# Splits on VectorE, shared gate splits, an early next segment and an earlier sum split in a one-core encoder layer

## The chip, the core and the metric

The kernel runs on one core of a Trainium2 chip. The metric is device time in microseconds (us) of one execution. The kernel before took 3487.39 us as the median of 3 runs (3483.35 to 3494.15).

The engines: TensorE (PE in the profile; its weight loads are PEld), VectorE (DVE), ScalarE (ACT), GpSimd (POOL) and SyncE (SP), which issues most DMAs. Each runs its own list of instructions in order; semaphores join them.

## The reference, cut to what matters

One encoder layer over 2048 tokens of width 1024, in float32:

```python
h = rmsnorm(x, ln_mix[layer])
z = h @ w_in[layer]
q_a, f_fw, f_bw, i_a, og_a, c_q, c_kv, k_rope, gate_a, gate_b = jnp.split(z, split_points, axis=-1)
...
o_hg = hgrn_direction(f_fw, lb_all[0, layer], False) + hgrn_direction(f_bw, lb_all[1, layer], True)
y_a = o_hg.reshape(B, S, HG_V).astype(x.dtype) @ w_oA[layer]
...
o_mla = block_dense_attention(qm, km, vm)     # 8 heads, softmax over all 2048 keys
y_b = o_mla @ w_oB[layer]
merged = jax.nn.sigmoid(gate_a) * y_a + jax.nn.sigmoid(gate_b) * y_b
x = x + merged @ w_out[layer]
x = x + hierarchical_moe(rmsnorm(x, ln_moe[layer]), ...)
x = x + (p[layer] @ w_ple_proj[layer]) * jax.nn.sigmoid(rmsnorm(x, ln_ple[layer]) @ w_ple_gate[layer])
```

`hgrn_direction` is a gated linear recurrence over the sequence, 4 heads of 128 x 128 state, run forwards and backwards.

## The kernel before

A product in full precision is made of three TensorE passes: each operand is split into a rounded high part and a low part (high x high, high x low, low x high). A split is one ScalarE copy (the high part) and one subtract (the low part) on VectorE or GpSimd. The order of every engine is written out by hand: inside `manual_schedule` an engine gets its instructions in the order in which the Python code emits them, and generators (`yield`) interleave strands of work.

**Stage 1, `stage_in`** (about 0 to 696 us) computes z but for the two branch gates. `todo` lists, for each of 4 token blocks (512 tokens), 5 groups of 288 columns done in 4 slots each (tokens by columns, `grp` is a number) and 6 groups of 256 columns done in 2 slots each (`grp` is None). A slot is 24 matmuls. Behind a slot's matmuls come: `post()` of the slot before (ScalarE, sometimes a VectorE product L346/L369 that reads PSUM), one step of every lane in `lanes` (`norm` of the next token block; `mla_block`, which normalises and rotates the latent q and k: lines L423 to L520), and in slot 0 `split_raw`, the split of the next group's weights in two halves (`whi` on ScalarE L269, `wlo` L270 on GpSimd). `load_raw` then starts the group after that.

**Stage 2, `hgrn` with `gates`** (about 696 to 1293 us). 16 segments (4 heads x 4 blocks of 512 tokens). `hgrn_levels` runs a segment in 8 steps: the start (`ff` L611 on ScalarE, `kk` L613 and `qq` L615 on VectorE, then matmuls L620/L621 into `h_ps`), and 7 levels. A level is: `h_ku` = copy of half of `kk` (ScalarE L627), `h_at` under a mask (VectorE L629), `kk` times `ff` in place (VectorE L632), half of the new `h_qq` (GpSimd L634), the other half copied (VectorE L635), `ff` pairs multiplied (VectorE L637), then matmuls L641. `hgrn_tail` (per segment) and `hgrn_forward` (per head: sums over the 4 segments, a reciprocal root in some 13 small VectorE steps, the scaled `h_so` L733, its transposes L737 into `h_pf`) are side strands; `side()` moves each of them by one step between a step's elementwise work and its matmuls.

`gates` is the filler: 64 units (4 token blocks x 16 column blocks of 128), each 24 matmuls L791 of 512 columns with its own weights `g_wr` loaded, split (`g_wh` on ScalarE, `g_wl` on GpSimd L768), and a sigmoid stored. It yields twice per GATE_STEP = 8 matmuls; each step of `hgrn` takes two yields. What is left of it runs on in the last `while tails` loop, in the start of `attention` (`run(n)`, between the first row maxima) and, in one piece, in `more()`.

**Stage 3, `attention`** (about 1361 to 2168 us; its first maxima run from 1314 us). 32 blocks (8 heads x 4 blocks of 512 queries) of 16 steps `kt`; a step is 3 score matmuls, 2 value matmuls, and 2 for the row maxima of the next block in every other step (`max_step`: 2 matmuls into `t_pm`, one PSUM buffer, then a VectorE reduction L947). Softmax sums of the first 12 key blocks are added up on GpSimd in `t_za` (L978, L980); `sums0` copies their high part to `t_zh` (ScalarE L1004) in step 13, `sums1` makes the low part `t_zl` (GpSimd L1009) in step 14, and `sums2` (step 15) multiplies both (L1015, L1016).

The merge, the experts and the last gate follow; the change does not touch them.

Of the kernel before, what the change touches and what calls it, by code (L numbers as in the profile page):

```python
# [174 lines left out]
def stage_in(tc, g, x, positions, ln_mix, w_in, qa_norm, kva_norm, w_uq, w_ukv, q_norm, k_norm, late):  # L175
# [5 lines left out]
    with ExitStack() as es:  # L181
# [199 lines left out]
        for at, (tb, c0, n, grp) in enumerate(todo):  # L381
# [5 lines left out]
            for i in range(2 if grp is None else 4):  # L387
# [18 lines left out]
                if i == 0 and at + 1 < len(todo):  # L406
                    ws = split_raw(raws, todo[at + 1][2], (nc.gpsimd if at + 2 < len(todo) else nc.vector,) * 2)
# [195 lines left out]
def hgrn_levels(tc, g, work, psum, hd, seg, loaded, z):  # L603

    nc = tc.nc
# [7 lines left out]
    nc.vector.tensor_scalar(kk, ff[:, 0:2], -1.0, 1.0, op0=OP.mult, op1=OP.add)  # L613
    qq = work.tile([128, 2, TB], F32, name="h_qq", bufs=5)
    nc.vector.tensor_tensor(qq, q[:, None, :].to_broadcast([128, 2, TB]), ff[:, 1:3], op=OP.mult)  # L615
    yield
    ps = psum.tile(SH, F32, name="h_ps")
    for c in range(HC):
        cs = slice(c * 128, (c + 1) * 128)
        nc.tensor.matmul(ps[:, c], kk[:, 0, cs], q[:, cs], start=True, stop=False)  # L620
        nc.tensor.matmul(ps[:, c], kk[:, 1, cs], q[:, cs], start=False, stop=True)  # L621
    yield
    at = work.tile(SH, F32, name="h_at")
    for lv in range(7):
# [10 lines left out]
        nc.vector.tensor_copy(others(qn, h, TB), others(qq, h, TB))  # L635
# [12 lines left out]
def hgrn_tail(tc, g, work, psum, hd, seg, z, st):  # L648
# [50 lines left out]
def hgrn_forward(tc, g, work, psum, hd, st):  # L699
# [4 lines left out]
    for seg in range(NTB):  # L704
# [29 lines left out]
        yield  # L734
        pt = psum.tile(SH, F32, name="h_pf", bufs=1)
# [8 lines left out]
def gates(tc, g, work, psum, w_in, n):  # L744

    nc = tc.nc
    todo = [(tb, cb) for tb in reversed(range(NTB)) for cb in range(2 * KC)]

    def raw(at, queue=nc.sync):
        if at >= len(todo):  # L750
            return None
        c0 = C_G + todo[at][1] * 128
# [18 lines left out]
    hx = None  # L771
# [9 lines left out]
    for at, (tb, cb) in enumerate(todo):
        if cb == 0:
            hx, hn = hn, []
        if cb in (4, 6, 8, 10) and tb:
            hn.append(row(tb - 1, len(hn) % 2, len(hn) // 2 * 4))
        pm = psum.tile([128, TB], F32, name="g_pm")
        wn = None
        for k in range(KC):
            a, b = (w[0][:, k], w[1][:, k]), (hx[k // 4 * 2][:, k % 4], hx[k // 4 * 2 + 1][:, k % 4])
            for i, (x, y) in enumerate(((a[0], b[0]), (a[0], b[1]), (a[1], b[0]))):  # L790
                nc.tensor.matmul(pm, x, y, start=k == 0 and i == 0, stop=k == KC - 1 and i == 2)  # L791
                count += 1
                if count % n == 0:
                    yield
                    if post:
                        post()
                        post = None
# [1617 lines left out]
```

## Time and profile before

| | us |
|---|---|
| median of 3 runs | 3487.39 (3483.35 to 3494.15) |
| the profiled execution | 3486.7, of which the span from first to last instruction is 3484.9 |
| TensorE busy | 3319.5 (95% of the span) |
| VectorE, ScalarE, GpSimd busy | 2489.9, 1985.3, 1435.8 |

Stages by their windows: 696 us for stage 1, 544 us for the 16 segments (696 to 1240), 121 us up to the first scores (1361), 807 us of attention, 1316 us for all that follows. [...]

### The profile page before, as it was taken

To read this page: it belongs to the slowest core of one execution; us is meant where nothing else is said; L and a number is where in the kernel's file an instruction comes from. 1 tells how busy PE (TensorE), PEld (TensorE's weight loads), DVE (VectorE), ACT (ScalarE), POOL (GpSimd) and SP (SyncE) were. 2 spreads that over 40 slices of the span, in tenths; PEclk is the share of its full clock that TensorE was granted. 3 is DMA by queue.
4 is the path that set the end of the run, shared out by engine and by line. 5 is a ranking of instruction groups with operands and counts; after the bars stand their busy time and mean duration, and the time that the engine had idled before them with its cause. 6 is when DMAs were issued, how large, how long until landed. Compare 5 with 4: busy or idle time off the path is not lost. (4 is left out here: it accounts for less than half of the span.)

```text
span 3484.9 us, 48287 instructions
## 1 busy us (share of the span) xinstructions
PE 3319.5 (95%) x16784; PEld 2784.7 (80%) x16784; DVE 2489.9 (71%) x4334; ACT 1985.3 (57%) x3522; POOL 1435.8 (41%) x973
## 2 busy tenths in 40 slices
PE   7999999999899899999999999999979999999899
PEld 6898989888787787777777777788868887888687
DVE  5545343388898854888888887665569998999775
ACT  5454544444444435888888887112228887888522
POOL 3333333255444435878777776000002222222244
PEclk9999999999999899999999999999989999999999
DMA  5645554554444354111101001876559899999642
GB/s 162 220 148 178 158 192 123 194 158 122 133 134 123 123 153 148 29 27 29 30 22 29 21 14 41 256 207 232 191 192 339 335 327 343 380 359 362 227 170 109
DMA packets 345077, 587.09 MB, mean 168 GB/s; under 512 B 57503, under 2 KB 220607, under 8 KB 332542
## 3 DMA queue, kind: packets, MB, share of 16 engines
q1 hardware_dynamic: 323726, 538.96, 46.4%
q0 software_dynamic: 20688, 43.45, 3.4%
q8 instruction: 133, 2.18, 0.3%
q10 hardware_dynamic: 416, 1.57, 0.1%
q14 instruction: 114, 0.93, 0.1%
HBM read 470.47 MB, written 146.93 MB: 177 GB/s over the span
## 5 line engine op out<-in xcount | busy, mean ns | idle before, releaser
L1919 DVE TENSOR_TENSOR e_wl<-e_raw,e_wh 128x1024 fp32r<-128x1024 f32 x384 | 459.7, 1221 | 47.9 <-ACT e_wh L1917 39.4
L980 POOL TENSOR_TENSOR t_za<-t_za,t_ph 128x512 f32<-128x512 f32 x320 | 416.0, 1300 | 47.8 <-ACT t_ph L972 34.8
L1917 ACT ACTIVATE e_wh<-e_raw 128x1024 fp32r<-128x1024 f32 x384 | 402.8, 1068 | 21.5 <-DMA e_raw<-in_w_dram 17.6
L270 POOL TENSOR_TENSOR wlo<-wraw,whi 128x1024 fp32r<-128x1024 f32 (+1 forms) x85 | 223.2, 2648 | 439.7 <-ACT whi L269 439.7
L947 DVE TENSOR_REDUCE t_mx<-t_pm 128x1 f32<-128x1024 f32 x256 | 313.4, 1224 | 118.2 <-PE t_pm L946 116.9
L985 DVE TENSOR_TENSOR t_pl<-t_ps,t_ph 128x512 fp32r<-128x512 f32 x512 | 341.9, 683 | 54.6 <-ACT t_ps L973 50.8
L972 ACT ACTIVATE t_ph<-t_ps 128x512 fp32r<-128x512 f32 x512 | 304.9, 596 | 111.9 <-PE t_ps L970 100.5
L791 PE MATMUL g_pm<-g_h,g_wh 128*128 128x512 f32 x1024 | 341.5, 407 | 1.9 <-ACT g_wh L767 1.9
L973 ACT ACTIVATE t_ps<-t_ps 128x512 f32<-128x512 f32 x512 | 303.3, 592 | 0.0
L1971 POOL DMA_INDIRECT d_y<-e_raw,sly x64 | 75.3, 1176 | 466.0 <-ACT e_raw L1969 404.6
L634 POOL TENSOR_TENSOR h_qq<-h_qq,h_ff 128x512 f32<-128x512 f32 x112 | 152.7, 1363 | 200.3 <-DVE h_ff L637 116.0
L791 PEld LDWEIGHTS g_pm<-g_h,g_wh 128*128 128x128 f32 x1024 | 194.6, 194 | 38.4 <-ACT g_wh L767 2.2
L768 POOL TENSOR_TENSOR g_wl<-g_wr,g_wh 128x1024 fp32r<-128x1024 f32 x63 | 153.9, 2443 | 141.1 <-ACT g_wh L767 133.7
L99 PE MATMUL e_pg<-e_wh,e_xh 128*128 128x512 f32 x512 | 208.9, 408 | 1.7 <-ACT e_wh L1917 1.2
L791 PE MATMUL g_pm<-g_h,g_wl 128*128 128x512 f32 x512 | 208.9, 408 | 1.6 <-POOL g_wl L768 1.1
L99 PE MATMUL pm<-whi,hh 128*128 128x288 f32 x640 | 198.4, 310 | 11.2 <-DVE qo L346 9.6
L968 PE MATMUL t_ps<-t_ql,t_kh 96*128 96x512 f32 x512 | 205.0, 400 | 2.0 <-DVE t_pl L985 2.0
L627 ACT ACTIVATE h_ku<-h_kk 128x512 f32<-128x512 f32 x112 | 75.6, 675 | 228.6 <-DVE h_kk L632 190.8
L100 PE MATMUL e_pg<-e_wl,e_xh 128*128 128x512 f32 x512 | 202.2, 395 | 2.9 <-DVE e_wl L1919 2.6
L101 PE MATMUL e_pg<-e_wh,e_xl 128*128 128x512 f32 x512 | 204.1, 399 | 0.5 <-DVE e_xl L1906 0.5
L997 PE MATMUL t_pa<-t_ph,vt 128*128 128x512 f32 x512 | 202.1, 395 | 0.0
L970 PE MATMUL t_ps<-t_qh,t_kh 97*128 97x512 f32 x512 | 202.0, 394 | 0.0
(452 smaller groups left out, 9356.9 us busy)
## 6 DMA issues: line engine op xcount, KB each, us to landing
e_raw<-in_w_dram SPq DMA_DIRECT2D x256, 512.0 KB
e_raw<-in_w_dram SPq DMA_DIRECT2D x64, 1024.0 KB
g_wr<-in_w_in_dram SPq DMA_DIRECT2D x62, 512.0 KB
wraw<-in_w_in_dram SPq DMA_DIRECT2D x48, 512.0 KB
wraw<-in_w_in_dram SPq DMA_DIRECT2D x40, 576.0 KB
d_g<-g_o SPq DMA_DIRECT2D x64, 256.0 KB
m_g<-d_g SPq DMA_DIRECT2D x64, 256.0 KB
p_y<-d_y SPq DMA_DIRECT2D x16, 1024.0 KB
```

What stands on the lines that cost most here:

```text
L99: nc.tensor.matmul(out, ah, bh, start=start, stop=False)
L101: nc.tensor.matmul(out, al, bh, start=False, stop=stop)
L270: e.tensor_tensor(lo[:, k:k + 4, :n], raw[:, :, :n], hi[:, k:k + 4, :n].bitcast(F32), op=OP.subtract)
L791: nc.tensor.matmul(pm, x, y, start=k == 0 and i == 0, stop=k == KC - 1 and i == 2)
L947: nc.vector.tensor_reduce(mx[n, i][:, j:j + 1], pm.rearrange("p a b -> p (a b)"), axis=AX, op=OP.max)
L968: nc.tensor.matmul(ps, kh[0:QK, ks], ql[0:QK], start=True, stop=False)
L972: nc.scalar.activation(ph, ps, AF.Exp)
L973: nc.scalar.activation(ps, ps, AF.Exp)
L980: nc.gpsimd.tensor_tensor(za[n], za[n], ph.bitcast(F32), op=OP.add)
L985: nc.vector.tensor_tensor(pl, p, ph.bitcast(F32), op=OP.subtract)
L1917: nc.scalar.activation(hi, raw, AF.Copy)
L1919: nc.vector.tensor_tensor(lo, raw, hi.bitcast(F32), op=OP.subtract)
```

## The change

1. `split_raw` becomes a generator of two steps and always subtracts on VectorE. In the 4-slot groups the first half is emitted in slot 0, the second in slot 1; in the 2-slot groups both in slot 0. At the start of the kernel the first group's second half and the second token tile's square sum are emitted earlier.
2. `gates` has a list `uses` of 40 weight blocks instead of 64: 12 column blocks used for the token blocks a and b together, then 4 for each of a, b, c, d alone, then 12 for c and d together. Rows of b are loaded at the start (by SP), those of c and d while the single ones run. GATE_STEP is 9, and both yields of a step are taken before `side()`.
3. `hgrn_levels` has more yields; the next segment's `ff`, `kk`, `qq` are emitted in steps 5, 6 and 7 of the segment before. Step 0 adds the two `kk` (VectorE) so that one matmul per block replaces the pair L620/L621. The other half of `h_qq` is copied on ScalarE. `hgrn_tail` gets a yield ahead of its products, `hgrn_forward` one between `h_so` and its transposes.
4. `sums0` and `sums1` move to steps 12 and 13.

```diff
-        def split_raw(raws, n, engines):
+        def split_raw(raws, n):
...
-            for raw, e, k in zip(raws, engines, range(0, KC, 4)):
+            for raw, k in zip(raws, range(0, KC, 4)):
                 nc.scalar.activation(hi[:, k:k + 4, :n], raw[:, :, :n], AF.Copy)
-                e.tensor_tensor(lo[:, k:k + 4, :n], raw[:, :, :n], hi[:, k:k + 4, :n].bitcast(F32), op=OP.subtract)
+                nc.vector.tensor_tensor(lo[:, k:k + 4, :n], raw[:, :, :n], hi[:, k:k + 4, :n].bitcast(F32), op=OP.subtract)
+                yield
             return hi, lo
...
                 if i == 0 and at + 1 < len(todo):
-                    ws = split_raw(raws, todo[at + 1][2], (nc.gpsimd if at + 2 < len(todo) else nc.vector,) * 2)
+                    part = split_raw(raws, todo[at + 1][2])
+                    next(part)
+                    if grp is None:
+                        ws = all_steps(part)
+                if i == 1 and grp is not None:
+                    ws = all_steps(part)
...
+    ks = work.tile([128, TB], F32, name="h_ku")
+    nc.vector.tensor_tensor(ks, kk[:, 0], kk[:, 1], op=OP.add)
     yield
     ps = psum.tile(SH, F32, name="h_ps")
     for c in range(HC):
         cs = slice(c * 128, (c + 1) * 128)
-        nc.tensor.matmul(ps[:, c], kk[:, 0, cs], q[:, cs], start=True, stop=False)
-        nc.tensor.matmul(ps[:, c], kk[:, 1, cs], q[:, cs], start=False, stop=True)
+        nc.tensor.matmul(ps[:, c], ks[:, cs], q[:, cs], start=True, stop=True)
...
-        nc.vector.tensor_copy(others(qn, h, TB), others(qq, h, TB))
+        nc.scalar.activation(others(qn, h, TB), others(qq, h, TB), AF.Copy)
...
             nc.vector.scalar_tensor_tensor(so[:, c], op[:, c], r[:, c:c + 1], so[:, c], op0=OP.mult, op1=OP.mult)
         yield
+        yield
         pt = psum.tile(SH, F32, name="h_pf", bufs=1)
...
-    todo = [(tb, cb) for tb in reversed(range(NTB)) for cb in range(2 * KC)]
+    a, b, c, d = reversed(range(NTB))
+    last = 2 * KC
+    uses = [(cb, (a, b)) for cb in range(last - 4)]
+    uses += [(cb, (t,)) for t in (a, b) for cb in range(last - 4, last)]
+    uses += [(cb, (t,)) for t in (c, d) for cb in range(4)]
+    uses += [(cb, (c, d)) for cb in range(4, last)]
...
     w, wr = parts(wr, nc.vector), wn
+    for i in range(4):
+        row(b, i)
     yield
...
         for step in range(8):
             next(lane)
-            for _ in range(5 if n == step == 0 else 1):
+            if step == 5 and n + 1 < len(segs):
+                nxt = begin(n + 1)
+            if step >= 5 and n + 1 < len(segs):
+                next(nxt[0])
+            for _ in range(6 if n == step == 0 else 2):
                 next(fill, None)
             side()
-            next(fill, None)
             next(lane, None)
...
-GATE_STEP = 8
+GATE_STEP = 9
...
+            if kt == 12:
+                sums0(n)
             if kt == 13:
-                sums0(n)
-            if kt == 14:
                 sums1(n)
```

What this moves, at three places. Stage 1, a 4-slot group, VectorE: two rotation steps of `mla_block` (L485 to L507, after the change L501 to L523; `kf` is what PE transposes next) with the `hl` splits of `norm` between them. Before:

```order
L206 TENSOR_TENSOR hl<-pt,hh 128x4x128 x2
L485 TENSOR_TENSOR qs<-qs,hr_y_4525 128x768
L486 TENSOR_TENSOR kf<-kf,hr_y_4525 128x8x64
L493 TENSOR_TENSOR ra<-qs,tc_899 128x256
L496 TENSOR_TENSOR rb<-qs,ts_900 128x8x16 x2
L498 TENSOR_TENSOR qs<-ra,rb 128x8x32
L502 TENSOR_TENSOR ka<-csb,tc_977 128x32
L504 TENSOR_TENSOR kb<-csb,ts_978 128x16 x2
L505 TENSOR_TENSOR ka<-ka,kb 128x32
L507 TENSOR_TENSOR kf<-ka,hr_y_4525 128x8x32
```

The same place after:

```order
L206 TENSOR_TENSOR hl<-pt,hh 128x4x128 x2
L270 TENSOR_TENSOR wlo<-wraw_4463,whi 128x4x256
L501 TENSOR_TENSOR qs<-qs,hr_y_4525 128x768
L502 TENSOR_TENSOR kf<-kf,hr_y_4525 128x8x64
L509 TENSOR_TENSOR ra<-qs,tc_899 128x256
L512 TENSOR_TENSOR rb<-qs,ts_900 128x8x16 x2
L514 TENSOR_TENSOR qs<-ra,rb 128x8x32
L518 TENSOR_TENSOR ka<-csb,tc_975 128x32
L520 TENSOR_TENSOR kb<-csb,ts_976 128x16 x2
L521 TENSOR_TENSOR ka<-ka,kb 128x32
L523 TENSOR_TENSOR kf<-ka,hr_y_4525 128x8x32
```

One half of a weight split (`wlo`) now stands in VectorE's row between the two rotations; it stood in GpSimd's before.

Stage 2, ScalarE, around the turn from one segment to the next (`h_op` and `h_qf` are a tail's copies, `g_o` and `g_wh` the gates'). Before:

```order
L691 ACTIVATE h_op<-h_po 128x512
L693 ACTIVATE h_qf<-h_qq 128x512
L627 ACTIVATE h_ku<-h_kk 128x512 x2
L809 ACTIVATE g_o<-g_pm 128x512
L767 ACTIVATE g_wh<-g_wr 128x1024
L627 ACTIVATE h_ku<-h_kk 128x512
L611 ACTIVATE h_ff<-h_sg,lb,lbc 128x512 x3
L627 ACTIVATE h_ku<-h_kk 128x512
L631 ACTIVATE h_at<-h_ps 128x512
```

After:

```order
L628 ACTIVATE h_ff<-h_sg,lb,lbc 128x512 x3
L714 ACTIVATE h_op<-h_po 128x512
L716 ACTIVATE h_qf<-h_qq 128x512
L649 ACTIVATE h_ku<-h_kk 128x512
L657 ACTIVATE h_qq<-h_qq 128x8x2x32
L846 ACTIVATE g_o<-g_pm 128x512
L804 ACTIVATE g_wh<-g_wr 128x1024
L649 ACTIVATE h_ku<-h_kk 128x512
L657 ACTIVATE h_qq<-h_qq 128x4x2x64
L846 ACTIVATE g_o<-g_pm 128x512
L649 ACTIVATE h_ku<-h_kk 128x512
L653 ACTIVATE h_at<-h_ps 128x512
```

`h_ff` of the next segment has moved three steps forward, and every level has a second ScalarE copy (L657), which waits for GpSimd's half of the same tile.

The start of attention, PE: the first row maxima (`t_pm`) of block 0 and the gate matmuls between them. Before:

```order
L791 MATMUL g_pm<-g_h,g_wl 128x512
L791 MATMUL g_pm<-g_h,g_wh 128x512
L946 MATMUL t_pm<-t_kh,t_qh 128x512 x2
L791 MATMUL g_pm<-g_h,g_wh 128x512
L791 MATMUL g_pm<-g_h,g_wl 128x512
L791 MATMUL g_pm<-g_h,g_wh 128x512 x2
```

After:

```order
L829 MATMUL g_pm<-g_h,g_wh 128x512 x2
L829 MATMUL g_pm<-g_h,g_wl 128x512
L993 MATMUL t_pm<-t_kh,t_qh 128x512 x16
L1002 MATMUL t_pb<-ident,mz_12566 97x128 x4
L993 MATMUL t_pm<-t_kh,t_qh 128x512 x6
L1015 MATMUL t_ps<-t_ql,t_kh 128x512
```

All of the gates' matmuls now stand ahead of the first maximum: 60 behind the last `h_pf` transposes, none behind the first `t_pm`. Before, 88 stood between those two, and 176 behind the first `t_pm`.

## Rows read from the trace of the kernel before

**Rows 1.** The page's first part: busy us of each engine, share of the span, instructions.
```profile
PE 3319.5 (95%) x16784; PEld 2784.7 (80%) x16784; DVE 2489.9 (71%) x4334; ACT 1985.3 (57%) x3522; POOL 1435.8 (41%) x973
```
**Rows 2.** [...]
```profile
30.00:696.00 666.00, 634.52 (x3712) 573.29 (x3712) 293.97 (x712) 303.28 (x647) 220.05 (x94) 0.97 0.52 171
696.00:1240.00 544.00, 501.72 (x2996) 441.08 (x2997) 464.58 (x802) 254.47 (x469) 262.62 (x157) 0.95 0.43 131
...
1361.00:2168.00 807.00, 781.88 (x3365) 619.27 (x3363) 662.76 (x923) 660.33 (x1220) 632.88 (x486) 1.00 0.11 29
```
**Rows 3.** What PE waited for from 30 to 696 us: us in all, times, the longest.
```profile
PE pt L515 <- DVE kf L507: 14.7, 4, 5.1
PE pm L99 <- DVE qo L346: 9.6, 5, 2.4
PE pt L436 <- DVE csb L427: 4.9, 1, 4.9
```
**Rows 4.** Timeline of single engines in stage 1: start, us taken, engine, line, what; in brackets the idle time ahead and who ended it. First VectorE's two scalings at the kernel's start, then GpSimd's two halves of a weight split at 268.88, VectorE's L493 beside them and again 9 us later alone, and PE's transposes of `kf`.
```profile
21.40 6.99 DVE L219 SCALAR_TENSOR_TENSOR xt<-xt,nx_r_y,gB 128x1024 f32<-128x1024 f32 x2
...
268.88 5.38 POOL L270 TENSOR_TENSOR wlo<-wraw,whi 128x1024 fp32r<-128x1024 f32 x2 [13.48 <-ACT whi L269]
...
269.37 2.62 DVE L493 TENSOR_TENSOR ra<-qs,tc 128x256 f32<-128x256 f32 x1
...
278.61 0.42 DVE L493 TENSOR_TENSOR ra<-qs,tc 128x256 f32<-128x256 f32 x1
...
280.90 0.97 PE L515 MATMUL pt<-ident,kf 128*96 128x128 f32 x7 [3.17 <-DVE kf L507]
```
**Rows 5.** Line L270, the low parts of the weights: ns min/median/max of one on GpSimd and of the few that stood on VectorE, first and last start.
```profile
L270 POOL TENSOR_TENSOR wlo<-wraw,whi x85: 2382/2662/3782, 10.7 to 661.9; 128x1024 fp32r<-128x1024 f32 x46, 128x1152 fp32r<-128x1152 f32 x39
...
L270 DVE TENSOR_TENSOR wlo<-wraw,whi x3: 1225/1226/1351, 10.6 to 673.0; 128x1024 fp32r<-128x1024 f32 x2, 128x1152 fp32r<-128x1152 f32 x1
```
**Rows 6.** Windows right behind a wait of PE, one in stage 1 and one in stage 2 (columns as in rows 2).
```profile
78.00:84.00 6.00, 3.79 (x15) 3.52 (x16) 4.86 (x21) 3.34 (x10) 0.00 (x0) 0.50 0.26 87
...
914.00:917.00 3.00, 3.00 (x14) 2.74 (x14) 2.37 (x7) 1.22 (x3) 0.74 (x1) 0.51 0.00 0
```
**Rows 7.** What PE waited for from 696 to 1262 us, the longest in total and the start of a segment.
```profile
PE h_pf L737 <- DVE h_so L733: 34.3, 12, 4.2
PE h_ps L620 <- PE h_pt L657: 1.7, 3, 0.7
```
**Rows 8.** Timeline of single engines around one of the twelve waits for `h_so`: GpSimd's gate split, VectorE beside it, PE.
```profile
905.96 2.38 POOL L768 TENSOR_TENSOR g_wl<-g_wr,g_wh 128x1024 fp32r<-128x1024 f32 x1 [2.87 <-ACT g_wh L767]
...
906.43 2.45 DVE L632 TENSOR_TENSOR h_kk<-h_kk,h_ff 128x512 f32<-128x512 f32 x1 [0.67 <-ACT h_ku L627]
...
913.74 1.26 PE L737 MATMUL h_pf<-ident,h_so 128*128 128x128 f32 x4 [4.19 <-DVE h_so L733]
```
**Rows 9.** Groups of instructions by line, 696 to 1240 us: count, busy us, mean ns of one, idle time ahead and what ended it.
```profile
L634 POOL TENSOR_TENSOR h_qq<-h_qq,h_ff 128x512 f32<-128x512 f32 x112 | 152.7, 1363 | 200.3 <-DVE h_ff L637 116.0 <-DVE h_qq L615 35.1 <-DVE h_fe L695 25.4
...
L768 POOL TENSOR_TENSOR g_wl<-g_wr,g_wh 128x1024 fp32r<-128x1024 f32 x45 | 110.9, 2464 | 81.8 <-ACT g_wh L767 74.6 <-DVE h_sb L682 3.5 <-DVE h_r_s L60 2.6
L627 ACT ACTIVATE h_ku<-h_kk 128x512 f32<-128x512 f32 x112 | 75.6, 675 | 228.6 <-DVE h_kk L632 190.8 <-DVE h_kk L613 25.2 <-PE h_ps L641 8.8
L635 DVE COPY h_qq<-h_qq 128x512 f32<-128x512 f32 x112 | 70.7, 631 | 5.0 <-POOL h_qq L634 5.0
...
L620 PE MATMUL h_ps<-h_q,h_kk 128*128 128x128 f32 x128 | 27.1, 296 | 2.5 <-PE h_pt L657 1.7 <-PE h_pf L737 0.8
```
**Rows 10.** PE's timeline where it never waits: the level matmuls of two successive steps with 8 gate matmuls between them, and two successive gate matmuls.
```profile
903.92 1.05 PE L641 MATMUL h_ps<-h_qq,h_ku 128*128 128x128 f32 x8
...
906.67 1.05 PE L641 MATMUL h_ps<-h_qq,h_ku 128*128 128x128 f32 x8
...
1354.64 0.39 PE L791 MATMUL g_pm<-g_h,g_wh 128*128 128x512 f32 x1
1354.87 0.39 PE L791 MATMUL g_pm<-g_h,g_wl 128*128 128x512 f32 x1
```
**Rows 11.** Attention: what PE waited for from 1361 to 2168 us (first row), then timelines at the end of one block: GpSimd's low part, PE's two products with high and low part and its next matmul.
```profile
PE t_pb L1016 <- POOL t_zl L1009: 22.3, 31, 1.1
...
1514.91 1.28 POOL L1009 TENSOR_TENSOR t_zl<-t_za,t_zh 128x512 fp32r<-128x512 f32 x1
...
1515.14 0.40 PE L1015 MATMUL t_pb<-t_zh,zo 128*128 128x512 f32 x1
1516.24 0.50 PE L1016 MATMUL t_pb<-t_zl,zo 128*128 128x512 f32 x1 [0.71 <-POOL t_zl L1009]
1516.58 0.40 PE L968 MATMUL t_ps<-t_ql,t_kh 96*128 96x512 f32 x1
```
**Rows 12.** Timelines at the start of attention: PE's last `h_pf` transposes, ScalarE's second key split and a gate split behind it, PE's first row maximum and VectorE's reduction of it.
```profile
1292.53 1.07 PE L737 MATMUL h_pf<-ident,h_so 128*128 128x128 f32 x4 [0.25 <-PE g_pm L791]
...
1303.42 0.62 ACT L912 ACTIVATE t_kh<-t_kr 96x512 fp32r<-96x512 f32 x1
...
1307.92 1.06 ACT L767 ACTIVATE g_wh<-g_wr 128x1024 fp32r<-128x1024 f32 x1 [2.72 <-DMA g_wr<-in_w_in_dram]
...
1314.83 0.62 PE L946 MATMUL t_pm<-t_kh,t_qh 96*128 96x512 f32 x2
...
1315.49 1.23 DVE L947 TENSOR_REDUCE t_mx<-t_pm 128x1 f32<-128x1024 f32 x1 [2.89 <-PE t_pm L946]
```

More of the change, by code (lines that the diff above doesn't have):

```diff
@@ L664, in hgrn_tail @@
         kts.append(kt)
+    yield
     for d in range(2):
@@ L774, in gates @@
         work.tile([128, KC, 128], F32R, name=name, bufs=2)
-    hn = [row(todo[0][0], j, k, nc.gpsimd) for k in (0, 4) for j in range(2)]
+    for i in range(4):
+        row(a, i, nc.gpsimd)
     wn = raw(1, nc.gpsimd)
@@ L778, in gates @@
     w, wr = parts(wr, nc.vector), wn
+    for i in range(4):
+        row(b, i)
     yield
     count, post = 0, None
[L781 to L786, printed above, removed]
-        wn = None
[L788 to L797, printed above, removed]
-                    if k >= 1 and wn is None and at + 1 < len(todo):
-                        wn, wr = parts(wr), raw(at + 2)
-                    yield
-        if wn is None and at + 1 < len(todo):
-            wn, wr = parts(wr), raw(at + 2)
-        w = wn
-        if post:
-            post()
-        def post(pm=pm, tb=tb, cb=cb):
-            o = work.tile([128, TB], F32, name="g_o", bufs=2)
-            nc.scalar.activation(o, pm, AF.Sigmoid)
-            nc.sync.dma_start(g.d_g[cb // KC][cb % KC][tb], o)
@@ new lines, in gates, with post @@
+    for at, (cb, tbs) in enumerate(uses):
+        wn = None
+        for tb, i in loads.get(at, ()):
+            row(tb, i)
+        for tb in tbs:
+            pm = psum.tile([128, TB], F32, name="g_pm")
+            for k in range(KC):
+                x, y = (w[0][:, k], w[1][:, k]), (hx[tb][k // 4 * 2][:, k % 4], hx[tb][k // 4 * 2 + 1][:, k % 4])
+                for i, (p, q) in enumerate(((x[0], y[0]), (x[0], y[1]), (x[1], y[0]))):
+                    nc.tensor.matmul(pm, p, q, start=k == 0 and i == 0, stop=k == KC - 1 and i == 2)
+                    count += 1
+                    if count % n == 0:
+                        yield
+                        if post:
+                            post()
+                            post = None
+                        if k >= 1 and wn is None and at + 1 < len(uses):
+                            wn, wr = parts(wr), raw(at + 2)
+                        yield
+            if wn is None and at + 1 < len(uses):
+                wn, wr = parts(wr), raw(at + 2)
+            if post:
+                post()
+            def post(pm=pm, tb=tb, cb=cb):
+                o = work.tile([128, TB], F32, name="g_o", bufs=2)
+                nc.scalar.activation(o, pm, AF.Sigmoid)
+                nc.sync.dma_start(g.d_g[cb // KC][cb % KC][tb], o)
+        w = wn
@@ L838, in end, with begin @@
             tails.append(hgrn_forward(tc, g, work, psum, hd, st))
+    def begin(n):
+        z = Ctx()
+        return hgrn_levels(tc, g, work, psum, *segs[n], loaded.pop(), z), z
+    nxt = begin(0)
+    for _ in range(3):
+        next(nxt[0])
     for n, (hd, seg) in enumerate(segs):
-        z = Ctx()
-        lane = hgrn_levels(tc, g, work, psum, hd, seg, loaded.pop(), z)
+        lane, z = nxt
         for step in range(8):
             next(lane)
-            for _ in range(5 if n == step == 0 else 1):
+            if step == 5 and n + 1 < len(segs):
+                nxt = begin(n + 1)
+            if step >= 5 and n + 1 < len(segs):
+                next(nxt[0])
+            for _ in range(6 if n == step == 0 else 2):
                 next(fill, None)
             side()
-            next(fill, None)
             next(lane, None)
@@ L853, in hgrn @@
     while tails:
-        next(fill, None)
+        for _ in range(2):
+            next(fill, None)
         side()
-        next(fill, None)
 HC = TB // 128
-GATE_STEP = 8
+GATE_STEP = 9
 def attn_consts(tc, g, pool):
```

33 lines of the change are left out of this document (24 added, 9 removed).

## The prediction

> **What bounds the kernel now.** First the page's busy shares: TensorE works 95% of the span, VectorE 71%, ScalarE 57%, GpSimd 41% [rows 1]. So only TensorE's idle time, its clock and its number of instructions can move the end. Next the windows by stage, since what limits differs [rows 2]. Stage 1 has 666 − 634.5 = 31.5 us of idle and a granted clock of 0.97; counting a stretch at mean clock c as (1 − c) of its length lost, that is 0.03 x 666 = 20 us. The segments have 544 − 501.7 = 42.3 us of idle and, at 0.95, 27 us of clock. Attention has 25 us of idle at 1.00. Then the tables of waits, which say for whom TensorE stood: in stage 1 for three VectorE results [rows 3], in the segments nearly only for `h_so` [rows 7], in attention for `t_zl` [rows 11]. [...] What follows attention is not changed and counts as nothing.
>
> **Stage 1: the splits on VectorE.** The waits for `kf`, `qo` and `csb` are 29.2 of the 31.5 us [rows 3]. The timelines say why VectorE was late [rows 4]: while GpSimd makes two halves of a split (5.38 us), VectorE's L493 takes 2.62 us, alone 0.42; PE then stands 3.17 us for `kf`. Removed are 85 GpSimd subtracts of a mean 2.66 us; added are 85 on VectorE, of which three stood there already at 1.23 us each [rows 5]. That is 104 us more on an engine busy for 294 of 666 [rows 2]: about 60% in the mean, so it has room, but not at every place. In the 4-slot groups the halves are emitted in two slots, so that at most 1.23 us stands ahead of a rotation, where the pair on GpSimd cost L493 alone 2.62 − 0.42 = 2.2 us. I take 6 us of idle as left, 31.5 − 6 = 25 us gained, and a clock of 0.99 (6 us lost, 14 gained): **−39**. The bounds: if only half of the idle and of the clock goes, −25; if all goes, −51. At the kernel's start the two scalings beside a GpSimd half take 6.99 us [rows 4]; with that half on VectorE this shrinks by some 4, but 1.23 is added and the first loads set the start as well: **−1** (0 to −3).
>
> **The segments.** In all twelve waits for `h_so` PE reaches the transposes L737 before VectorE has finished `h_so`, up to 4.2 us before [rows 7]. `h_so` and its transposes are successive steps of the side strand, with one step of the segment between; VectorE's level work in front of it is stretched by a gate split on GpSimd (L632 takes 2.45 us beside it [rows 8]). The added `yield` puts one more step in between. A step is 544/128 = 4.25 us in the mean; the longest wait is 4.2. So most go whole; some come back since steps get shorter: 34.3 → 9, **−25** (bounds: −15 with half, −34). Preparing the next segment in steps 5 to 7 takes the chain `ff`, `kk`, `qq` out of the turn; PE lost little there [rows 7]: **−2**. The clock goes from 0.95 to 0.99: 27 → 6, **−21** (0 if waits spring up elsewhere, −27). One of each pair of matmuls L620/L621 goes; L621 issues as many as L620, 128 [rows 9]. Their pitch: two level steps lie 2.75 us apart, of which 8 gate matmuls at 0.23 take 1.84 [rows 10], which leaves 0.116 for each of the 8 level matmuls. 128 x 0.11 = **−14** (−10 to −20). GATE_STEP 9 instead of 8 brings 128 x 0.23 = 29 us of gate work forward from behind; it is work in any case, so it lengthens the segments and shortens what follows, and costs nothing in the sum. The 24 weight blocks that are no longer loaded and split take nothing off PE: their splits lay on GpSimd and ScalarE, whose idle time is not the bound.
>
> Against that, the copy of the other half goes from VectorE (0.63 us) to ScalarE (some 0.68, as L627 takes [rows 9]). The trace has no such ScalarE copy, but it shows that the VectorE copy, which waits for the same GpSimd product, stood only 5.0 us in 112 [rows 9]. ScalarE executes its list in order, and behind the copy queue the gates' `g_o` and `g_wh`, and `h_at` and `h_ku` of the next level, for which PE waits. GpSimd has the 1.36 us product of each level and a 2.46 us gate split; of these splits some 32 instead of 45 fall into the segments now. If a third of the 32 holds the copy up by half a us that reaches PE, **+4** (0 to +40; the upper end is 32 x 1.23, half a split each). Sum of the segments: −25 − 2 − 21 − 14 + 4 = **−58**, bounds about −25 and −80.
>
> The rows of b are four more loads of 1 MB on SP ahead of the gates' next weights. PE needs them after the 24 gate matmuls of the first a-unit, 5.5 us. The nearest row is a wait for gate weights behind loads, 2.72 us [rows 12]. I take **+1** (0 to +3).
>
> **Attention's end of a block.** `t_zl` is made in 1.28 us; PE starts L1015, then L1016 1.10 us later and its next matmul 0.34 after that, where successive matmuls of 512 columns lie 0.23 apart [rows 10, 11]. So one block loses 0.87 + 0.11 = 0.98, and over 31 waits 22.3 us are idle by the table [rows 11]; 31 x 0.95 = 29 takes in the slowing around the wait. Sums one step earlier gain 807/512 = 1.58 us, more than the longest wait of 1.1. No other engine's row is late then: **−29** (−22 to −31).
>
> **Attention's start.** Here the change costs. Before, 176 gate matmuls stood behind the first `t_pm` and filled the time in which VectorE reduces one maximum while PE may not write the next (one PSUM buffer). After, none does. A pair takes 0.66 us on PE and 1.23 on VectorE [rows 12], 1.9 us with PE's share 0.46: eleven pairs, 11 x 1.45 = 16 us idle. The 60 gate matmuls ahead of it (60 x 0.23 = 13.8 us) still cover the loads, since from the last `h_pf` to the second key split it took 1303.42 − 1292.53 = 10.9 us [rows 12]. With about 4 us for slower matmuls behind it: **+20** (+14 to +28).
>
> Behind waits of this length PE's rows showed 0.50 [rows 6]. [...]
>
> **The sum.** −39 − 1 − 58 + 1 − 29 + 20 = −106, against the profiled execution's 3486.7 us; the median of the runs, 3487.4, is the same within 0.7. 3486.7 − 106 = 3381, taken as **3382**. The own range comes from the terms' bounds, not all at one end: 3345 to 3405.
>
> **Rivals.**
> *B, the wait only moves in the segments.* PE no longer stands at `h_pf`, but at `h_ps`: the ScalarE copy behind GpSimd's product delays `h_ku` and `h_at`. For it: every level now hands from GpSimd to ScalarE, 112 times, and a gate split of 2.46 us can stand ahead of the product. Against: the 5.0 us of the VectorE copy [rows 9]. Idle and clock then stay; only the dropped matmuls count, −15 instead of −58: 3382 + 43 = **3425**.
> *C, VectorE's list eats stage 1's gain.* The splits now stand in VectorE's list between rotations and `qo`, so PE waits for the same names as before. For it: VectorE is what PE waits for there [rows 3]. Against: 1.23 us against 2.2 us and more before. Stage 1 gives 0: 3382 + 39 = **3421**.
> *D, better.* The start of attention costs 5 (the reductions of the first block overlap PE's other work), stage 1 gives 48, the segments 78: 3382 − 15 − 9 − 20 = **3338**.
> *E, slower than before: the level's loop becomes the bound.* Product (GpSimd), copy of the other half, `h_ku` (ScalarE) and the split that falls into a quarter of the levels: 1.36 + 0.68 + 0.68 + 2.46 x 32/112 = 3.4 us by rows 9. PE's own step is 9 x 0.23 + 8 x 0.116 = 3.0 by rows 10, some 3.7 with the side strands' matmuls (today 501.7/128 = 3.9 [rows 2], the dropped matmuls and the lower clock in it). So the loop has 0.3 to spare. If the product grew to 2.85 us by running beside VectorE's work (L632 shows such growth [rows 8]), a level takes 4.9 us, 0.65 over today's 4.25: 112 x 0.65 = +73, of which the 29 us of gate work brought forward come back, and PE waits in every level, so at a clock of 0.90 another 0.05 x 617 = +31. With −39 − 1 + 1 − 29 + 20 = −48 elsewhere: 3486.7 − 48 + 73 − 29 + 31 = **3514**. It decides from 4.25 + (48 + 29 − 31)/112 = 4.66 us a level. Against: rows 9 have the product at 1.36 in the mean, beside that very work.
> [...] The 5.0 us of the copy on VectorE show how seldom it waited there.
>
> **How the numbers follow.** Forecast 64%, B 15%, C 8%, D 7%, E 6%. B and C together would be 3464, still faster by 0.6%. A measurement of this kernel can tell about 0.3% (10.5 us) from no change; E gives slower 4%, and 2% with what lies between it and B with C gives 4% for no change; faster 92%. The range takes in B and C and the upper bounds of the forecast, and below most of D: **3340 to 3430**.
>
> **What would show it.** In the profile after: waits for `kf`, `qo` and `csb` under 10 us and 0.99 in stage 1; `h_pf` under 12 us and 0.99 in the segments, which should last 544 − 58 + 29 = 515 us with 9 gate matmuls in each step; no row L1016 among attention's waits; a row for `t_pm` waiting for `t_mx` at attention's start, ten times 1.4 us. Wrong would be the forecast if a wait of PE for `h_ps` or `h_ku` over 15 us appears (B, E), if `kf` stays over 20 us (C), or if mean `h_qq` on GpSimd exceeds 2 us (E).

## The result and the profile after

The changed kernel takes 3390.07 us (median of 4 runs, 3387.27 to 3393.04), the kernel before beside it 3488.83: a ratio of 0.9717, 95% interval 0.9698 to 0.9736. The profiled execution has a span of 3390.4 us, 94.5 less than before.

The stages on PE's timeline, each from its first matmul to that of the next (attention to its last product with `t_zl`). Of the gate matmuls 204 (46.9 us at 0.23) moved from behind the last `h_pf` to ahead of it; they are counted in neither stage.

| stage | before | after | difference | predicted |
|---|---|---|---|---|
| start and stage 1, to the first gate matmul | 696.65 | 657.01 | −39.6 | −40 |
| segments, from the first gate matmul to the last `h_pf` | 595.9 | 594.3, less 46.9 | −48.5 | −57 |
| attention's start, to the first scores | 68.0 | 41.8 and 46.9 | +20.6 | +20 |
| attention | 807.0 | 776.6 | −30.4 | −29 |
| what follows, unchanged | 1317.4 | 1320.8 | +3.4 | 0 |

Windows of the changed kernel: stage 1, the segments, the loop's end, attention's start, attention. The columns, those of [rows 2] and [rows 6] too, are from and to, length, busy us (and instructions) of PE, PEld, DVE, ACT and POOL, then TensorE's granted clock as a share of full speed, the busy share of the DMA engines and GB/s.

```profile
30.00:656.50 626.50, 619.52 (x3710) 558.73 (x3709) 321.59 (x794) 301.43 (x646) 6.51 (x10) 1.00 0.56 183
656.50:1187.00 530.50, 504.80 (x3008) 444.98 (x3009) 403.46 (x704) 312.38 (x575) 242.04 (x146) 0.98 0.40 126
1187.00:1265.40 78.40, 78.40 (x371) 65.38 (x370) 26.96 (x91) 23.94 (x59) 13.27 (x6) 1.00 0.42 122
1265.40:1293.00 27.60, 12.87 (x27) 6.27 (x26) 14.21 (x17) 5.08 (x7) 3.58 (x2) 0.59 0.68 216
1293.00:2070.00 777.00, 775.90 (x3367) 623.78 (x3365) 663.55 (x924) 662.40 (x1218) 635.92 (x486) 1.00 0.10 25
```

Beside [rows 2]: stage 1's idle time went from 31.5 to 7.0 us and its clock from 0.97 to 1.00. The segments' went from 42.3 to 25.7, their clock from 0.95 to 0.98. The one window with a low clock is new: attention's start.

PE's waits in the changed kernel, from 30 to 640 us (against [rows 3]) and from 640 to 1180 us (against [rows 7]); in attention no row for `t_zl` is left (against [rows 11]).

```profile
PE pm L99 <- DVE qo L357: 4.1, 5, 1.3
PE pm L99 <- ACT csb L352: 0.6, 1, 0.6
...
PE h_ps L643 <- issue: 13.3, 4, 4.6
PE h_po L711 <- DVE h_sb L705: 7.7, 9, 1.9
PE g_pm L829 <- DMA g_h<-d_ht: 2.6, 2, 1.9
```

The wait of 34.3 us for `h_so` is gone, and two others are in its place, 21.0 us together. The profile names no engine for the first ("issue"), so the timelines of GpSimd, VectorE and PE at one of the four have to tell. It is a segment's turn, that is, the place where one segment ends and the next starts:

```profile
1043.41 2.00 POOL L656 TENSOR_TENSOR h_qq<-h_qq,h_ff 128x512 f32<-128x512 f32 x1 [1.31 <-DVE h_ss L753]
...
1043.38 0.17 DVE L60 TENSOR_SCALAR h_r_s<-h_ss 128x4 int32<-128x4 int32 x1
1043.59 1.85 DVE L62 TENSOR_SCALAR h_r_s<-h_r_s 128x4 int32<-128x4 int32 x1
1045.47 0.16 DVE L67 TENSOR_TENSOR h_r_a<-h_r_s 128x4 f32<-128x4 f32 x1
...
1047.24 1.14 DVE L756 SCALAR_TENSOR_TENSOR h_so<-h_op,h_r_y,h_so 128x128 f32<-128x128 f32 x4
1048.30 0.68 DVE L638 TENSOR_TENSOR h_ku<-h_kk 128x512 f32<-128x512 f32 x1
...
1049.08 2.04 PE L643 MATMUL h_ps<-h_q,h_ku 128*128 128x128 f32 x8 [4.59 <-issue]
```

The sum of the two `kk` (L638) stands on VectorE behind the whole reciprocal root (the small rows from L60 on) and `h_so`, some 5 us of work in one step; it ends at 1048.98 (1048.30 + 0.68) and PE starts 0.1 us later. The eight records then take 2.04 us, where eight of that size take 1.05 in [rows 10], so PE runs slowly behind the wait: the granted clock of these 2.04 us is 0.50, as in [rows 6].

Attention's start after: what PE waited for (1265 to 1293 us), then PE and VectorE (against [rows 12]):

```profile
PE t_pm L993 <- DVE t_mx L994: 13.9, 9, 3.3
...
1265.42 0.63 PE L993 MATMUL t_pm<-t_kh,t_qh 96*128 96x512 f32 x2
1269.39 0.70 PE L993 MATMUL t_pm<-t_kh,t_qh 96*128 96x512 f32 x2 [3.33 <-DVE t_mx L994]
1271.40 1.22 PE L993 MATMUL t_pm<-t_kh,t_qh 96*128 96x512 f32 x2 [1.31 <-DVE t_mx L994]
1273.94 1.22 PE L993 MATMUL t_pm<-t_kh,t_qh 96*128 96x512 f32 x2 [1.32 <-DVE t_mx L994]
...
1272.66 1.23 DVE L994 TENSOR_REDUCE t_mx<-t_pm 128x1 f32<-128x1024 f32 x1 [1.12 <-PE t_pm L993]
```

From the third on a pair of maxima starts every 2.54 us (once 2.91, with four transposes between), with a reduction of 1.23 between, and takes 1.20 to 1.22 us instead of 0.63: the granted clock is 1.00 from 1265.4 to 1270.4 us and 0.50 from there to 1293. The first wait is 2.0 us longer than the others, since VectorE makes the low part of the keys (`t_kl` L960, from 1266.82 to 1268.1) ahead of its first reduction.

### The profile page after: what moved, and what is told of

It is laid out like the page before. It is cut to its first block, busy times and chain, and to the rows that moved or that the text cites. A ratio compares the mean times of both kernels' runs of the same rounds, so it can differ in the third digit from the quotient of the medians.

```text
span 3390.4 us, 47885 instructions
## 1 busy us (share of the span) xinstructions
PE 3276.8 (97%) x16656; PEld 2755.7 (81%) x16656; DVE 2445.8 (72%) x4323; ACT 2028.8 (60%) x3610; POOL 1164.1 (34%) x864
## 5 line engine op out<-in xcount | busy, mean ns | idle before, releaser
L656 POOL TENSOR_TENSOR h_qq<-h_qq,h_ff 128x512 f32<-128x512 f32 x112 | 159.7, 1426 | 164.1 <-DVE h_ff L659 81.8
L829 PEld LDWEIGHTS g_pm<-g_h,g_wh 128*128 128x128 f32 x1024 | 185.4, 191 | 36.7 <-DMA g_h<-d_ht 3.3
L270 DVE TENSOR_TENSOR wlo<-wraw,whi 128x1024 fp32r<-128x1024 f32 (+1 forms) x88 | 111.2, 1281 | 135.4 <-ACT whi L269 135.2
L829 PE MATMUL g_pm<-g_h,g_wl 128*128 128x512 f32 x512 | 202.1, 395 | 0.5 <-DVE g_wl L805 0.5
L1016 PE MATMUL t_ps<-t_qh,t_kl 96*128 96x512 f32 x512 | 202.3, 395 | 0.0
L1045 PE MATMUL t_pb<-t_pl,vt 128*128 128x512 f32 x512 | 200.9, 392 | 0.0
```

The costliest lines, as they stand in the source:

```text
L829: nc.tensor.matmul(pm, p, q, start=k == 0 and i == 0, stop=k == KC - 1 and i == 2)
```

## Experiments

All are edits of the changed kernel, timed beside the kernel before on the same chip. The last column is from the first gate matmul to the first scores. The medians are of 4 runs each, the last column is of the one profiled execution.

| edit | median us | ratio to before (95%) | segments and attention's start |
|---|---|---|---|
| none | 3390.07 | 0.9717 (0.9698 to 0.9736) | 636.1 |
| e1 weight splits on GpSimd | 3417.73 | 0.9801 (0.9785 to 0.9817) | 634.0 |
| e2 no added step | 3390.68 | 0.9720 (0.9704 to 0.9736) | 634.6 |
| e3 copy on VectorE | 3393.70 | 0.9732 (0.9716 to 0.9748) | 637.0 |
| e4 sums late | 3426.25 | 0.9821 (0.9804 to 0.9837) | 640.5 |
| e5 8 gate matmuls | 3379.76 | 0.9698 (0.9675 to 0.9720) | 624.8 |
| e6 early sum | 3390.02 | 0.9726 (0.9703 to 0.9749) | 636.2 |
| e7 early sum, later products | 3384.36 | 0.9711 (0.9688 to 0.9734) | 632.4 |
| e8 e7 with 8 | 3377.24 | 0.9693 (0.9670 to 0.9717) | 623.4 |
| e9 root in two steps | 3384.17 | 0.9700 (0.9684 to 0.9717) | 629.0 |
| e10 e9 with 8 | 3376.13 | 0.9684 (0.9667 to 0.9700) | 619.3 |
| e11 e2, half of the filler behind | 3401.24 | 0.9752 (0.9735 to 0.9768) | 645.4 |
| e12 pair of matmuls; one slot | 3397.89 | 0.9746 (0.9729 to 0.9762) | 632.5 |

The edit in e4 lies behind the segments, and they came out 4.4 us longer there: differences of that size between two profiles are not read. The start and stage 1, to the first gate matmul, lie between 655.7 and 660.5 us in the eleven traces that have it as in the changed kernel (657.0).

**e1.**
```diff
-                nc.vector.tensor_tensor(lo[:, k:k + 4, :n], raw[:, :, :n], hi[:, k:k + 4, :n].bitcast(F32), op=OP.subtract)
+                e.tensor_tensor(lo[:, k:k + 4, :n], raw[:, :, :n], hi[:, k:k + 4, :n].bitcast(F32), op=OP.subtract)
...
-                    part = split_raw(raws, todo[at + 1][2])
+                    part = split_raw(raws, todo[at + 1][2], (nc.gpsimd if at + 2 < len(todo) else nc.vector,) * 2)
```


> The changed kernel with the low parts of stage 1's weights back on GpSimd (still in two slots of a 4-slot group). Theory (GpSimd's subtract slows the VectorE operations beside it): the waits of PE for kf, qo and csb come back, 20 to 30 us, and the clock of stage 1 falls to 0.97 or 0.98; 3410 to 3425. Rival (the spread over two slots made the gain, whatever the engine): stage 1 stays at 627 us, 3388 to 3398.

The theory holds for the waits and the time. PE's waits from 30 to 656 us:
```profile
PE pt L531 <- DVE kf L523: 14.4, 4, 5.0
PE pm L99 <- DVE qo L357: 5.1, 2, 2.7
PE pt L452 <- DVE csb L443: 1.9, 1, 1.9
```
and the rotation's product (ns min/median/max of one), in the changed kernel and here:
```profile
L509 DVE TENSOR_TENSOR ra<-qs,tc x16: 415/417/419, 106.4 to 624.5; 128x256 f32<-128x256 f32 x16
```
```profile
L509 DVE TENSOR_TENSOR ra<-qs,tc x16: 416/420/2626, 110.1 to 650.3; 128x256 f32<-128x256 f32 x16
```
The `kf` waits are those of [rows 3]: with `qo` and `csb` 21.4 us. The clock from 30 to 656.5 us came out at 0.99, above the 0.97 or 0.98 expected. The first gate matmul comes at 680.69 us, 23.7 later: so much of the 39.6 is the engine alone. (The profiled execution is the fastest of e1's four; the medians lie 27.7 apart.)

**e12.** Two edits, in stages that are read apart.
```diff
-                    next(part)
-                    if grp is None:
-                        ws = all_steps(part)
-                if i == 1 and grp is not None:
                     ws = all_steps(part)
...
-    ks = work.tile([128, TB], F32, name="h_ku")
-    nc.vector.tensor_tensor(ks, kk[:, 0], kk[:, 1], op=OP.add)
...
-        nc.tensor.matmul(ps[:, c], ks[:, cs], q[:, cs], start=True, stop=True)
+        nc.tensor.matmul(ps[:, c], kk[:, 0, cs], q[:, cs], start=True, stop=False)
+        nc.tensor.matmul(ps[:, c], kk[:, 1, cs], q[:, cs], start=False, stop=True)
```


> The changed kernel with two edits in stages that are read apart by their windows: both halves of every weight split of stage 1 on VectorE in one slot, and the pair of matmuls per block in step 0 instead of the sum of the two kk. Theory: in stage 1 a pair of 2.5 us on VectorE makes kf or qo late by a little, 3 to 8 us more than 626.5; in the segments 128 more matmuls of 0.11 are 14 us, and the 13 us of waits at L643 go to other places: 3402 to 3412. Rival (the sum's wait cost as much as the matmuls that it saved): segments within 4 us of before that edit; and stage 1 within 2 us: 3386 to 3394.

In stage 1 the first gate matmul comes at 662.90, 5.9 us later, as the theory had it. That is 2.4 us behind the latest of the eleven traces above, so two slots are worth some 2 to 7 us; waits for `kf` are back (30 to 656 us), which the changed kernel doesn't have:
```profile
PE pt L527 <- DVE kf L519: 3.3, 3, 1.3
```
In the segments the rival was right: with the pair back they are no longer than without it (632.5 against 636.1). The median lies between the two expectations. PE's longest wait there, and a window as long as the changed kernel's that starts, as that one does, just ahead of the first gate matmul, show the exchange:
```profile
PE h_po L706 <- DVE h_sb L700: 11.2, 16, 1.9
```
```profile
662.50:1193.00 530.50, 515.52 (x3153) 456.23 (x3154) 393.28 (x690) 313.62 (x578) 238.12 (x146) 0.99 0.40 126
```
PE is busy 515.5 instead of 504.8 us, but idle 15.0 instead of 25.7. What the sum saved in matmuls it cost in waits for it.

**e2, e11.** Without the step between `h_so` and its transposes; in e11 one of the two filler yields also stands behind `side()`, as before the change (the same in the last `while tails` loop).
The first piece is e2, both are e11:
```diff
         yield
-        yield
         pt = psum.tile(SH, F32, name="h_pf", bufs=1)
...
-            for _ in range(6 if n == step == 0 else 2):
+            for _ in range(5 if n == step == 0 else 1):
                 next(fill, None)
             side()
+            next(fill, None)
```


> The changed kernel without the second yield between h_so and its transposes. Theory (the yield hides VectorE's lateness, except at a segment's turn, where the same lateness now stands as a wait for the sum of the two kk): h_pf waits of 20 to 34 us come back, the 13 us at L643 mostly vanish with them, the segments' clock falls to 0.96; 3402 to 3418. Rival (the waits only change their name): 3385 to 3397.

> The changed kernel without the added step before the transposes, and with one of the two filler yields behind side() again, as before the change. Theory (the step adds nothing, and what halved the waits for h_so is that the whole filler now stands ahead of the transposes, 4 or 5 matmuls of 0.23 more, some 1.1 us each time): the h_pf waits rise from 16.6 to 28 or more and the total to 3400 to 3412. Rival (the waits fell since VectorE has less to do at a turn): h_pf stays under 20 us, 3386 to 3396.

The wait of PE for `h_so` in e2 (656 to 1190 us), then in e11 (656 to 1265 us):
```profile
PE h_pf L760 <- DVE h_so L756: 16.6, 12, 3.7
```
```profile
PE h_pf L760 <- DVE h_so L756: 22.0, 10, 3.7
```
In e2 16.6 us stand for the 21.0 at L643 and L711, and the time is the same: the added step moved the wait and gained nothing, against my theory. Without the step the wait had halved already, from 34.3 to 16.6. In e11 22.0, not the 28 expected, came back, and the total rose by 10.6 us over e2, as the theory had it: taking the whole filler ahead of `side()` is worth that, a part of the halving and of the clock (0.97 in e11's segments, 0.98 in e2's).

How it gains is not shown. The expectation had the filler as cover for VectorE, but VectorE also has less to do. Its product of `kk` and `ff` before the change, in e2 and in e11 (16 segments; the second number behind the first bar is the mean ns of one):
```profile
L632 DVE TENSOR_TENSOR h_kk<-h_kk,h_ff 128x512 f32<-128x512 f32 x112 | 129.9, 1160 | 32.3 <-PE h_ps L621 30.4 <-ACT h_ku L627 1.7
...
L654 DVE TENSOR_TENSOR h_kk<-h_kk,h_ff 128x512 f32<-128x512 f32 x112 | 111.1, 992 | 27.0 <-ACT h_ku L649 27.0
...
L654 DVE TENSOR_TENSOR h_kk<-h_kk,h_ff 128x512 f32<-128x512 f32 x112 | 134.0, 1197 | 32.1 <-ACT h_ku L649 31.7
```
It took 1.16 us before, takes 0.99 in e2 and again 1.20 in e11. Where GpSimd has no instruction beside it, it takes 0.75 in the mean before and 0.74 in the changed kernel (41 and 66 of the 112). That the place of the filler also sets how much of VectorE's work GpSimd's stands beside is my reading of these means; the overlap was not counted in e2 and e11.

**e6, e7, e9.** e6 emits the sum beside `qq`, a step earlier. e7 also has a second `yield` in `hgrn_tail` between the states `h_sb` and the products that read them. e9 leaves the sum and cuts the root. First e6, then e9:
```diff
     nc.vector.tensor_tensor(qq, q[:, None, :].to_broadcast([128, 2, TB]), ff[:, 1:3], op=OP.mult)
-    yield
-
     ks = work.tile([128, TB], F32, name="h_ku")
     nc.vector.tensor_tensor(ks, kk[:, 0], kk[:, 1], op=OP.add)
     yield
+
+    yield
...
-        r = rsqrt_small(nc, work, ss, [128, HC], "h_r")
+        root = rsqrt_steps(nc, work, ss, [128, HC], "h_r")
+        for _ in range(6):
+            next(root)
+        yield
+        while True:
+            try:
+                next(root)
+            except StopIteration as last:
+                r = last.value
+                break
         for c in range(HC):
             nc.vector.scalar_tensor_tensor(so[:, c], op[:, c], r[:, c:c + 1], so[:, c], op0=OP.mult, op1=OP.mult)
         yield
-        yield
         pt = psum.tile(SH, F32, name="h_pf", bufs=1)
```


> The changed kernel with the sum of the two kk emitted one step earlier, next to qq, so that it stands on VectorE ahead of the reciprocal root and h_so of the side strand. Theory (what PE waits for at L643 is that sum behind the root's small steps): the 13 us at L643 go, and since the first level's matmuls need only a ScalarE copy, nothing takes their place: 3374 to 3381. Rival (VectorE's lateness itself is the limit, and shows at the next row that needs it, L651 or L654 and then L663): 3386 to 3394.

> As the kernel with the early sum, and one more step between the states h_sb of a tail and the products that read them. Theory: the 7.7 us at L711 go too, 3367 to 3375. Rival (the wait moves on): as the kernel with the early sum or slower.

> The changed kernel with the reciprocal root cut in two: its first six small VectorE steps stay where they are, the rest and h_so come one step of the segment later, in the step that the change left empty; the transposes stay. Theory (what moves from place to place in the earlier runs is one burst of 5 us on VectorE in one step, root and h_so together; cut in two it fits): the 21 us of waits at L643 and L711 fall under 10 and nothing takes their place, 3374 to 3382. Rival (VectorE is late by the amount of work around a turn, not by the burst): 3386 to 3394.

PE's longest waits in the segments, of e6, e7 and e9:
```profile
PE h_po L711 <- DVE h_sb L705: 11.1, 12, 2.0
PE h_pf L761 <- DVE h_so L756: 5.5, 4, 2.0
```
```profile
PE h_ps L663 <- ACT h_ku L649: 15.8, 15, 2.1
PE h_pf L745 <- DVE h_sf L740: 3.7, 3, 1.7
```
```profile
PE h_ps L643 <- issue: 11.4, 5, 2.4
PE h_pf L769 <- DVE h_so L765: 2.4, 2, 1.3
PE h_po L711 <- DVE h_sb L705: 2.2, 4, 0.8
```
e6: 13.3 us at L643 went, and most of it came back, 3.4 more at L711 and 5.5 at the transposes; the time is the same, so the rival holds. e7: again, 15.8 us now at L663; 5.7 us are gained, less than the theory had and more than the rival. e9: the burst cut in two leaves 16.0 us of the 21.0, none over 2.4; the last column is 7.1 us shorter, and the median lies between the two expectations. The burst is a part of the lateness, not all of it.

**e3.**
```diff
-        nc.scalar.activation(others(qn, h, TB), others(qq, h, TB), AF.Copy)
+        nc.vector.tensor_copy(others(qn, h, TB), others(qq, h, TB))
```


> The changed kernel with the copy of the other half of h_qq back on VectorE. Theory (VectorE's list is what PE waits for at L643 and L711, so 112 x 0.63 = 71 us more in it make these waits longer): 3394 to 3405. Rival (the ScalarE copy behind GpSimd's product makes h_ku and h_at late): the waits at L643 and L711 shrink from 21 us to under 12, 3375 to 3387.

L643 waits 15.7 us, L711 6.9: 22.6 against 21.0. The waits didn't shrink, so the rival falls; but 71 us more of work on VectorE made them only 1.6 us longer, so the theory isn't shown either, and the 3.6 us of the medians are at the edge of what can be told. How much VectorE has to do in all is then not what makes it late at a turn.

**e4.**
```diff
-            if kt == 12:
+            if kt == 13:
                 sums0(n)
-            if kt == 13:
+            if kt == 14:
                 sums1(n)
```


> The changed kernel with the attention sums back at steps 13 and 14. Theory (the 1.1 us wait for t_zl at every block's end is the whole gain of attention): 22 us of waits at the product with t_zl come back, 3415 to 3421. Rival (attention is shorter because of something else, such as GpSimd's or the DMA queues' state at its start): under 10 us, 3390 to 3400.

The wait is back as in [rows 11], and attention lasts 807.0 us again; the total is a little above what was expected, with the 4.4 us ahead of attention. PE's wait in attention:
```profile
PE t_pb L1063 <- POOL t_zl L1056: 21.9, 31, 1.1
```

**e5, e8, e10.** `GATE_STEP = 8`, alone, with e7 and with e9.

> The changed kernel with 8 gate matmuls for each step of the segments instead of 9, so that some 128 more of them are left for the end of the loop and the start of attention. Theory (attention's start is short of filler between a row maximum and the next: 14 us idle and a clock of 0.59): the start's waits for t_mx fall under 4 us, the segments' waits grow by some 3 us: 3370 to 3380. Rival (the start waits for its loads or for the late clock whatever stands between, or the segments need the ninth matmul as cover): 3387 to 3400.

> The last two edits and 8 gate matmuls for each step. Theory (the three are independent, since they lie in different places): the sum of what they give alone, 3350 to 3362. Rival (fewer gate matmuls take the cover from the segments, where waits come back): no better than the best of them.

> The same with 8 gate matmuls for each step. Theory: both gains, 3360 to 3370. Rival (with less filler the segments wait again): 3376 to 3384, as with 8 gate matmuls alone.

The window of attention's row maxima in e5:
```profile
1244.40:1281.00 36.60, 36.60 (x164) 30.15 (x164) 14.24 (x16) 6.03 (x10) 8.46 (x4) 1.00 0.29 88
```
The theory of e5 holds: no idle time, clock 1.00, 10.3 us gained. The segments wait more, and by more than the 3 us expected: from the first gate matmul to the last `h_pf` PE is idle 35.7 us instead of 25.2, with L643 at 14.4, L711 at 8.6, and `h_ku` at L663 at 3.8, which had no wait. With gate matmuls counted at 0.23, the ninth one spares the segments 11.3 us (605.6 against 594.3 at the same gate work) and costs attention's start 22.5 (5.5 against 28.0). e8 misses its sum by far: what e7 gave (5.7 us alone) is mostly not there, 2.5 us below e5. e10's median lies where its rival had it; its last column is 5.5 us shorter than e5's, little over what can be read. It has the lowest median here, 0.33% of before below the changed one.

## Why the prediction came out as it did

The time was predicted at 3382 and is 3390; the terms of the sum, by its own steps:

- **Stage 1** (−39 −1, measured −39.6). Right, and for its reason: e1 brings the waits for `kf` back with the engine alone, and rival C falls. The engine is 23.7 us of it, 27.7 by the medians. The other 12 to 16 are in e1 too, so they come from the two slots and the earlier emission at the start; the prediction took the slots only as a reason for the 6 us left. With the splits on VectorE the slots are some 2 to 7 us (e12). The start was not undone by itself.
- **Attention's end of a block** (−29, measured −30.4). Right; e4 returns all of it. The waits did not bring the clock down here: it was 1.00 over the 807 us with the 31 waits of at most 1.1 us [rows 2, 11].
- **Attention's start** (+20, measured +20.6). Right in size. Its own split was 16 us idle and 4 for slower matmuls; the window has 14.7 idle, and pairs of 1.22 instead of 0.63 us. No run shows the 4 us, an estimate of the prediction: [rows 6] have their 0.50 and 0.51 behind waits of 4.9 and 4.2 us. What the trace after shows is 0.50 from 1270.4 us on, with waits of 1.3 us between the pairs; nine of the eleven pairs stand there, mostly 2.54 us apart where the second and the third start 2.01 apart, so I estimate the slowing at 9 x 0.53 = 5 us. The gate matmuls ahead did not cover all, by the 2.0 us of the first wait. e5 shows that the missing filler is the cause.
- **The segments** (−58 and +1 for the rows of b, measured −48.5): the step that was mis-sized. By resource, the window's idle time fell by 16.6 us where −25 − 2 + 4 = −23 was forecast, and the clock's loss by 0.05 x 544 − 0.02 x 530.5 = 16.6 where −21 was forecast (the two digits of the clock leave some 4 us open). The term for `h_pf` took it that the added step gains what the transposes no longer wait. It gains nothing (e2): VectorE is as late as without it, and the next reader waits, the sum at a turn or the products with `h_sb`. The prediction's rival B had a wait that only moves, but named ScalarE's copy as its cause. The wait for `h_ps` that it gave as a sign of being wrong came to 13.3 us, under the 15 that it named, and from VectorE's root; of its other signs, 0.98 and 530.5 us stand where 0.99 and 515 were expected.
- **The dropped matmuls** (−14). Shown to be worth nothing in the end (e12): the sum that replaces them is one more VectorE row behind the root, and the prediction priced the matmuls that go but not the row that comes. (By rows 10 a level matmul is 0.91 / 8 = 0.114 us, not 0.116; no sum changes by it.)
- **The ScalarE copy** (+4). No loss was seen, rather 0 to 4 us gained (e3). Of the gate splits 34 fell into the segments where 32 were expected. The loop through GpSimd (rival E) did not take over: the product took 1.43 us in the mean, 1.36 before [rows 9].
- **The rows of b** (+1): 2.6 us of waits for `g_h` in two places, in the segments' sum.
- **The unchanged part** (0) came out 3.4 us longer, 1320.8. It lies between 1313.4 and 1324.6 in the twelve edits, around the 1317.4 before, so no effect of the change can be read.

That the segments came within 9 us of their forecast is in part luck. Of the forecast's terms the added step and the dropped matmuls, −25 and −14, are each worth nothing in the end. In their place stand two things that it had at nothing: the filler ahead of `side()`, some 11 us (e11), and the ninth gate matmul, some 11 us in the segments (e5), of which the prediction said that it costs nothing in the sum.

Open is what makes up the other half of the 48.5 us, if those two add up, which no run tells. The copy, the added step and the sum for the dropped matmuls are near none of it. That leaves the preparation of the next segment and the shared gate splits (34 on GpSimd in the segments, 45 before), which were not undone one by one. The prediction gave the first 2 us and the second nothing, though it read from [rows 8] that a gate split on GpSimd stretches VectorE's work (L632 took 2.45 us beside one). That one of them is worth more is argued from what is left, not shown.

## What to carry to other kernels

A wait that PE has for a late engine isn't always gained by putting a step between: look at what stands next in that engine's list. Here moving the readers of one burst gained nothing (e2, e6) or 5.7 us (e7), cutting the burst 5.9 (e9), and 71 us of work that the change took off the engine elsewhere left the waits within 1.6 us (e3). A filler is best kept for the place where nothing else can run; here the ninth gate matmul in each step spared the segments some 11 us and cost attention's start some 22, where the clock was 0.59 with it and 1.00 without it (e5). Before work is moved off the bound engine, see whether what replaces it stands behind a burst on another.

## What the hardware showed

In the changed kernel a VectorE instruction of 128x4 elements took 1.85 us beside a GpSimd product and ended with it (1043.59 + 1.85 = 1045.44 and 1043.41 + 2.00 = 1045.41 us), where the same took 0.17 at its median. In the segments and the loop behind them (ns min/median/max, line L62):

```profile
L62 DVE TENSOR_SCALAR h_r_s<-h_r_s x16: 169/170/1887, 818.6 to 1247.7; 128x4 int32<-128x4 int32 x16
```
Five of these sixteen overlap a GpSimd product; they took 1.14 to 1.89 us, and each ended 0.02 to 0.03 us behind it. The other eleven took 0.17. So even a row as small as this ended, in these five cases, only when GpSimd's product did.

TensorE's clock fell in e11 behind waits of no more than 1.41 us, with 0.63 to 0.73 us of work between them. It was 1.00 from 1187.00 to 1252.50 us and 0.88 from there to 1293.00. The second to the fourth pair of row maxima at attention's start:

```profile
1279.01 0.70 PE L993 MATMUL t_pm<-t_kh,t_qh 96*128 96x512 f32 x2 [1.41 <-DVE t_mx L994]
1281.03 0.73 PE L993 MATMUL t_pm<-t_kh,t_qh 96*128 96x512 f32 x2 [1.32 <-DVE t_mx L994]
1283.08 1.22 PE L993 MATMUL t_pm<-t_kh,t_qh 96*128 96x512 f32 x2 [1.31 <-DVE t_mx L994]
```

From the fourth pair on each takes 1.20 to 1.22 us, as the pairs of the changed kernel at its granted clock of 0.50. The first, at 1276.98, took 0.63 us, and from 1240 us up to it PE waited for nothing: gate matmuls stood there without a gap.
